# RWKV stage of a hybrid decoder layer: which engine makes the low parts and the second copy, and which bank holds the bonus product

## The chip, the cores and the metric

The kernel runs on one core of a Trainium2 chip. The metric is the device time of one execution in microseconds. Before the change the median of 3 runs is 2224.1 us (2221.66 to 2224.29).

## The reference

One layer of a decoder on a sequence of 1024 tokens with 1024 channels, in float32:

- One input projection `x @ w_in`. Its columns feed RWKV-7 time mixing (8 heads of 64), a sparse attention (8 query heads) and two merge gates of 1024 channels each.
- Time mixing, per head and per token t, with a 64x64 state: `sa = state @ a_t`; `state = state * w_t + sa b_t^T + v_t k_t^T`; `y_t = state @ r_t`. Then a norm per head, and a bonus is added: the sum over the head of `r * k * r_k`, times v.
- Both branches are projected, multiplied by their sigmoid gates, added and projected again; residual and layer norm.
- Cross-attention into 256 memory tokens; residual and layer norm. A gated feed-forward of width 2816 with a convolution of width 3; residual and layer norm.

```
sa = jnp.einsum('bhvk,bhk->bhv', state, a_t)
state = (state * w_t[:, :, None, :] + sa[..., None] * b_t[:, :, None, :]
         + v_t[..., None] * k_t[:, :, None, :])
return state, jnp.einsum('bhvk,bhk->bhv', state, r_t)
```

## The kernel before

**Matmuls in three parts.** Large products run in a reduced float32 format on TensorE. Each operand is split into a high and a low part, and `mm3` (line 194) adds three matmuls: high by high, high weights by low activations, low weights by high activations. `split` (199) makes the parts: ScalarE copies the source into the high part, VectorE subtracts it from the source for the low part. `wload` (211) streams a weight tile this way: a DMA into `raw` (one buffer), then `split` into `wh` and `wl` (two buffers each, so the next load is split as soon as the load before the present one has been used up). `wload` is used in all stages.

**The RWKV stage** (lines 563 to 960) works on four pairs of heads (`hp`) and two halves of the sequence, so on eight units. A half has 8 chunks of 64 tokens. For each unit:

- `operands` (646): decay and key factors. The matmuls `vs` (norm sums), `pw` and `pa` (small projections) and `bc` (the norm brought back, from the tile `w`) feed VectorE, ScalarE and GpSimd. Then the matrix `LT`, and a substitution of 15 steps on VectorE (L729, L730) that inverts its 16x16 blocks.
- `couplings` (746): products `gb` and `gk` masked by VectorE into `GB` and `AMR`; transposes `tr`; and the bonus product `pbo`, which VectorE multiplies by v into `BV`.
- `inverse` (809): the 64x64 inverse from the 16x16 blocks.
- `recurrence` (855): chunk by chunk, `x` on TensorE, copied to `XS` by VectorE; `sa` (the solved rows) on TensorE, whose two halves of 64 partitions are copied to `SV`, one by VectorE (866) and one by ScalarE (867); `z` on TensorE; and the next state `ZV` by VectorE (876), which the next `x` needs.
- `outputs` (879): `psy`, the norm (`vs`, `bc` again) and the bonus.

**Work that fills TensorE.** `large` (512) is a generator for the 13 column pieces of the projection that this stage needs (`prj`) and the 16 pieces of the gates (`gt`). Each piece is a load of 128x1024 and 2 x 8 steps of `mm3`, and the next piece is loaded ahead. The last gates run in the stage of the sparse attention.

**The order.** TensorE's order in this stage is written out by hand: tasks yield an assumed TensorE time and an assumed wait, and a loop (950 to 960) takes the first ready one of recurrences, outputs, inverses, couplings, operands and, last, `large`. The other engines' orders come from a scheduler that works from assumed times; the steps of recurrences and inverses are marked as urgent for it. Every engine then works in its own order, and waits by semaphores.

**PSUM banks** are handed out in turn within a role (563 on): role s has banks 2, 3 and 6 and serves `operands` and `couplings`; role o has bank 7 alone and serves `outputs`; b and c serve inverse and recurrence; g the filling matmuls.

Of the kernel before, what the change touches and what calls it, by code (L numbers as in the profile page):

```python
# [10 lines left out]
F32 = mybir.dt.float32  # L11
# [115 lines left out]
def layer_kernel(ctx: ExitStack, tc, I, out, cst):  # L127
# [42 lines left out]
    def pss(name="pss"):  # L170
        return bank("s", name)
# [4 lines left out]
    def pso(name="pso"):  # L176
        return bank("o", name)
# [18 lines left out]
        PE.matmul(o, lh, rl, start=False, stop=False)  # L196
        PE.matmul(o, ll, rh, start=False, stop=stop)  # L197

    def split(src, h, l):
        S.activation(h, src, AF.Copy)  # L200
        V.tensor_sub(l, src, h.bitcast(F32))  # L201

    class W:
        def __init__(self, ku):
# [3 lines left out]
            u, q = divmod(k, self.ku)  # L208
            return self.h[u][:, q, c:c + m], self.l[u][:, q, c:c + m]

    def wload(pieces, kt=8):

        n = sum(p.shape[1] for p in pieces)
        w = W(min(kt, WUNIT // n))
        for k0 in range(0, kt, w.ku):
            ku = min(w.ku, kt - k0)
            wp = in_turn("w", cur["w"])
            raw = wp.tile([P, ku, n], F32, tag="raw", bufs=1, name="raw")
            h = wp.tile([P, ku, n], F32R, tag="wh", bufs=2, name="wh")
            l = wp.tile([P, ku, n], F32R, tag="wl", bufs=2, name="wl")  # L220
            o = 0
            for p in pieces:
                m = p.shape[1]
                SP.dma_start(raw[:, :, o:o + m], p[k0 * P:(k0 + ku) * P].rearrange("(k p) n -> p k n", p=P))
                o += m
            split(raw, h, l)
            w.h.append(h)
            w.l.append(l)
        return w
# [282 lines left out]
    def large():  # L512

        def load():
            while pq and not may_load(*pq[0]) and not gq:
                yield 0, 0.5
            if pq and may_load(*pq[0]):
                c = pq.pop(0)
                col0 = c[1] * RC + c[0] * P
            elif gq:  # L520
                c = gq.pop(0)
                col0 = GATE0 + c * P
            else:
                return None
            return c, wload([win[:, col0:col0 + P]])

        ahead = yield from load()
        while ahead:
            c, w = ahead
            ahead = yield from load()  # L530
            gate = isinstance(c, int)
            if not gate:
                hp, j = c
                while not may_project(hp, j):
                    yield 0, 0.5
                dst = [LO[:, 0:HALF], LO[:, HALF:T]] if j == 3 else [ex(f"X{a}{j}") for a in range(2)]
                Xs[c] = dst
                last = sm.tile([P, 1], F32, name="last", tag="last", bufs=4)
            for half in range(2):
                ps = pg("gt" if gate else "prj")  # L540
                for k in range(8):
                    mm3(ps, *w.at(k, 0, P), *xT.mov(k, half), k == 0, k == 7)
                    if k < 7:
                        yield L_DENSE, 0, True
                if gate:
                    t = cur["st"].tile([P, HALF], F32, tag="gst", name="gst", bufs=1)
                    S.activation(t, ps, AF.Tanh, scale=0.5)
                    S.dma_start(gscr[c * P:(c + 1) * P, half * HALF:(half + 1) * HALF], t)
                else:
                    shifted(ps, dst[half], j * 4 + hp, half, last)  # L550
                    if half:
                        if j == 3:
                            S.activation(LO[0:64, :], LO[0:64, :], AF.Tanh)
                        projected.add(c)
                yield L_DENSE, 0, False
# [190 lines left out]
    def couplings(me):  # L746

        u, (hp, half) = units[me], divmod(me, 2)
        Xr, E3, ET, BH, KH, BB, KB_, TMP = u.operands
        Xv = Xs[hp, 2][half]  # L750
        AMR = k8("AMR")
        for h, rw in enumerate(rows_h):
            G.tensor_tensor(AMR[rw, :, 1, h, :], r8(Xr[rw]), r8(ET[rw]), op=OP.mult)
            S.activation(AMR[rw, :, 0, h, :], r8(E3[rw]), AF.Copy)

        GB, KS, SV, ZV = k2("GB"), k4("KS"), k4("SV"), k4("ZV")
        u.AMR, u.GB, u.KS, u.SV, u.ZV = AMR, GB, KS, SV, ZV
        if half == 0:
            for h, rw in enumerate(rows_h):
                G.memset(ZV[rw, 0, h, :], 0.0)  # L760
        yield 0, 5.5
        ps = pss("gb").rearrange("p (c t) -> p c t", t=CH)
        for c in range(NC8):
            for h, rw in enumerate(rows_h):
                PE.matmul(ps[rw, c], BH[rw, c * CH:(c + 1) * CH], AMR[rw, c, 1, h, :], start=True, stop=True)
        V.tensor_tensor(GB, ps, bc(gmask[:, CH:P], NC8), op=OP.mult)
        for j in range(2):
            ps = pss("gk").rearrange("p (c a t) -> p c a t", a=2, t=CH)
            for ci in range(4):
                c = 4 * j + ci  # L770
                for h, rw in enumerate(rows_h):
                    PE.matmul(ps[rows_h[1 - h], ci], KH[rw, c * CH:(c + 1) * CH], AMR[rw, c, :, h, :], start=True, stop=True)
            for h in range(2):
                rx = rows_h[1 - h]
                m = gmask[rx].rearrange("p (a t) -> p a t", a=2)[:, None].to_broadcast([64, 4, 2, CH])
                V.tensor_tensor(AMR[rx, 4 * j:4 * j + 4, :, h, :], ps[rx], m, op=OP.mult)
        yield 2.9, 1.0

        for src, flip, dst in ((Xv, 1, ZV), (BB, 0, KS), (KB_, 1, KS)):
            ps = pss("tr").rearrange("p (c n) -> p c n", n=P)  # L780
            for c in range(4):
                PE.transpose(ps[:, c, :], src[:, c * P:(c + 1) * P], ident)
            if src is Xv:

                mv = sm.tile([P, 4, 2], F32, name="vm", tag="vm", bufs=2)
                V.tensor_reduce(mv, ps.rearrange("p c (h d) -> p c h d", h=2), axis=AX.X, op=OP.add)
            for h in range(2):
                ro = rows_h[1 - h] if flip else rows_h[h]
                for q, rq in enumerate(rows_h):
                    o, v = dst[ro, q:NC8:2, h, :], ps[rq, :, h * 64:h * 64 + 64]  # L790
                    if src is Xv:
                        m = mv[rq, :, h][:, :, None].to_broadcast([64, 4, 64])
                        V.scalar_tensor_tensor(o, m, -1.0 / 64, v, op0=OP.mult, op1=OP.add)
                    else:
                        S.activation(o, v, AF.Copy)
                if src is Xv:
                    G.tensor_copy(SV[ro, :, h, :], ZV[ro, :, h, :])
            yield 0.5, 0.8
        yield 0, 2.5
        if me >= 2:  # L800
            while not outputs_[me - 2].done:
                yield 0, 0.5
        u.BV = ec("BV")
        ps = pss("pbo")
        PE.matmul(ps, ones, TMP, start=True, stop=True)
        V.scalar_tensor_tensor(u.BV, ps, 64.0, Xv, op0=OP.mult, op1=OP.mult)
        yield 1.1, 0
# [47 lines left out]
    def recurrence(i):  # L855
        u, (hp, half) = units[i], divmod(i, 2)
        AMR, EE, KS, SV, ZV, WC = u.AMR, u.EE, u.KS, u.SV, u.ZV, u.WC
        for c in range(NC8):
            ps = bank("c", "x")
            PE.matmul(ps[:, 0:P], pair(AMR[:, c, 0]), pair(ZV[:, c]), start=True, stop=True)  # L860
            XS = sm.tile([P, P], F32, name="XS", tag="XS", bufs=2)
            V.tensor_copy(XS, ps[:, 0:P])
            yield 0.35, 0.8
            ps = bank("c", "sa")
            PE.matmul(ps[:, 0:P], pair(EE[:, c]), XS, start=True, stop=True)
            V.tensor_copy(SV[0:64, c, 0, :], ps[0:64, 0:64])
            S.activation(SV[64:128, c, 1, :], ps[64:128, 64:128], AF.Copy)
            yield 0.25, 1.4
            if not (half == 1 and c == NC8 - 1):
                ps = bank("c", "z")  # L870
                PE.matmul(ps[:, 0:P], pair(KS[:, c]), pair(SV[:, c]), start=True, stop=True)
                while c == NC8 - 1 and not couplings_[i + 1].done:
                    yield 0, 0.5
                for h, rw in enumerate(rows_h):
                    dst = ZV[rw, c + 1, h, :] if c < NC8 - 1 else units[i + 1].ZV[rw, 0, h, :]
                    V.scalar_tensor_tensor(dst, ZV[rw, c, h, :], WC[rw, c, :], ps[rw, h * 64:h * 64 + 64], op0=OP.mult, op1=OP.add)
                yield 0.25, 1.2
# [657 lines left out]
```

## Time and profile before

| | before |
|---|---|
| median of 3 runs | 2224.1 us |
| the profiled execution, its own time | 2223.49 us |
| span of the profiled execution | 2221.7 us |
| TensorE busy in the span | 2131.7 us (96%) |
| VectorE busy | 1232.4 us (55%) |
| ScalarE busy | 889.2 us (40%) |
| GpSimd busy | 475.0 us (21%) |

The span goes from the first to the last instruction; the execution's own time is 1.8 us longer. Busy is the time in which an engine has an instruction in work. In the rows further down, PE is TensorE, DVE VectorE, ACT ScalarE, POOL GpSimd. Matmuls overlap their neighbours, so a row's duration is longer than the distance to the next row.

### The profile page before, as it was taken

The page shows a single profiled execution, that of the slowest core. Times are in us where ns is not written, and L with a number is a line of the kernel's source. Part 1 is how long each engine was busy: PE and PEld are TensorE (multiplying, and loading weights), DVE is VectorE, ACT ScalarE, POOL GpSimd, SP SyncE. Part 2 cuts the span into 40 slices and gives each one's busy share as a digit, 9 for nine tenths or more (in the row PEclk, how much of TensorE's full clock was granted, in tenths as well). Part 3 has the DMA queues.
Part 4 walks back from the last instruction along what each step waited for, and adds up shares of the span by engine and source line. Part 5 has one row for each costly group of instructions (what it writes and reads, how often), then busy time and mean ns, then how long its engine had stood idle before and what let it go on. Part 6 is the DMA issues. An engine that isn't in the chain of part 4 may idle for free.

```text
span 2221.7 us, 31651 instructions
## 1 busy us (share of the span) xinstructions
PE 2131.7 (96%) x12301; PEld 1706.0 (77%) x12301; DVE 1232.4 (55%) x2416; ACT 889.2 (40%) x1441; POOL 475.0 (21%) x544
## 2 busy tenths in 40 slices
PE   9989999999999899999899999999999999999997
PEld 7978777777778667756678877788888888888886
DVE  3422576777652787888656535275444434344447
ACT  3433443544533576776523424142322313132232
POOL 2112231333300244444422101030100101000013
PEclk9999999999999999999999999999999999999999
DMA  6544112121223321112252313111111111111102
GB/s 206 152 150 124 49 24 56 36 52 32 62 59 94 110 66 45 42 45 68 72 189 86 123 38 114 39 39 57 38 48 48 54 42 57 39 57 57 57 29 86
DMA packets 196659, 157.91 MB, mean 71 GB/s; under 512 B 49061, under 2 KB 164766, under 8 KB 196510
## 3 DMA queue, kind: packets, MB, share of 16 engines
q1 hardware_dynamic: 184798, 139.10, 21.2%
q10 hardware_dynamic: 11136, 14.68, 2.0%
q0 software_dynamic: 576, 2.10, 0.3%
q8 instruction: 98, 1.61, 0.3%
q14 instruction: 51, 0.42, 0.1%
HBM read 125.86 MB, written 29.98 MB: 70 GB/s over the span
## 4 chain that ended last, share of the span: by engine, by line
PE 47%; DVE 5%; ACT 2%; DMA 1%; issue 1%; POOL 0%; SPq 0%; ACTq 0%; DVEq 0%; POOLq 0%
PE up L196 7%; PE up L197 7%; PE up L195 7%; PE dn L195 4%; PE dn L197 4%; PE dn L196 4%; PE op L195 2%; PE op L197 1%; PE op L196 1%; PE xq L195 1%; PE xq L196 1%; PE xq L197 1%; DVE acc L1334 1%; ACT acc L1333 1%; DVE bs L1327 1%
## 5 line engine op out<-in xcount | busy, mean ns | idle before, releaser
L200 ACT ACTIVATE wh<-raw 128x1024 fp32r<-128x1024 f32 (+1 forms) x160 | 168.8, 1055 | 474.9 <-PE dn L197 138.1
L201 DVE TENSOR_TENSOR wl<-raw,wh 128x1024 fp32r<-128x1024 f32 (+1 forms) x160 | 198.1, 1239 | 282.5 <-ACT wh L200 281.5
L196 PE MATMUL up<-nTl,wh 128*128 128x512 f32 x704 | 276.5, 393 | 0.0
L197 PE MATMUL up<-nTh,wl 128*128 128x512 f32 x704 | 276.4, 393 | 0.0
L195 PE MATMUL up<-nTh,wh 128*128 128x512 f32 x704 | 276.4, 393 | 0.0
L1458 DVE SCALAR_TENSOR_TENSOR cv<-up,pv,cv 128x511 f32<-128x511 f32 (+1 forms) x176 | 131.5, 747 | 145.4 <-ACT cv L1456 143.4
L1482 POOL TENSOR_TENSOR cv<-cv 128x512 f32<-128x512 f32 x44 | 56.8, 1291 | 630.9 <-DVE cl L1462 413.5
L196 PEld LDWEIGHTS up<-nTl,wh 128*128 128x128 f32 x704 | 132.3, 188 | 29.6
L195 PEld LDWEIGHTS up<-nTh,wh 128*128 128x128 f32 x704 | 132.2, 188 | 29.6
L197 PEld LDWEIGHTS up<-nTh,wl 128*128 128x128 f32 x704 | 132.2, 188 | 29.6
L1106 POOL TENSOR_TENSOR pl<-pe,ph 128x512 fp32r<-128x512 f32 x87 | 114.3, 1317 | 161.3 <-ACT ph L1105 97.3
L195 PE MATMUL dn<-wh,gT 128*128 128x512 f32 x352 | 138.1, 393 | 0.2 <-ACT wh L200 0.2
L197 PE MATMUL dn<-wh,gT 128*128 128x512 f32 x352 | 137.5, 391 | 0.0
L196 PE MATMUL dn<-wl,gT 128*128 128x512 f32 x352 | 136.9, 389 | 0.0
L1493 DVE SCALAR_TENSOR_TENSOR acc<-acc,dn 128x512 f32<-128x512 f32 x96 | 65.5, 686 | 95.5 <-PE dn L197 94.9
L1456 ACT ACTIVATE cv<-up,pv 128x512 f32<-128x512 f32 x88 | 68.5, 778 | 117.2 <-PE up L197 117.2
L195 PE MATMUL gt<-xTh,wh 128*128 128x512 f32 x256 | 113.0, 441 | 0.5 <-DVE nm L1074 0.5
L197 PE MATMUL gt<-xTh,wl 128*128 128x512 f32 x256 | 102.3, 399 | 0.0
L196 PE MATMUL gt<-xTl,wh 128*128 128x512 f32 x256 | 101.9, 398 | 0.0
L1335 POOL TENSOR_TENSOR acc<-acc,lngb 128x1024 f32<-128x1024 f32 x21 | 50.4, 2401 | 206.0 <-DVE acc L1334 129.8
L1105 ACT ACTIVATE ph<-pe 128x512 fp32r<-128x512 f32 (+1 forms) x148 | 90.2, 627 | 6.9 <-POOL macc L1223 4.6
L195 PE MATMUL prj<-xTh,wh 128*128 128x512 f32 x208 | 90.5, 435 | 2.2 <-ACT wh L200 2.2
(365 smaller groups left out, 5092.2 us busy)
## 6 DMA issues: line engine op xcount, KB each, us to landing
raw<-in_ffn_w_up_dram SPq DMA_DIRECT2D x88, 256.0 KB
raw<-in_w_in_dram SPq DMA_DIRECT2D x33, 512.0 KB
raw<-in_ffn_w_down_dram SPq DMA_DIRECT2D x22, 512.0 KB
gscr<-gst ACTq DMA_DIRECT2D x32, 256.0 KB
rawn<-nst SPq DMA_DIRECT2D x16, 256.0 KB
raw<-in_xa_wk_dram SPq DMA_DIRECT2D x8, 512.0 KB
raw<-in_xa_wv_dram SPq DMA_DIRECT2D x8, 512.0 KB
gl<-gscr SPq DMA_DIRECT2D x16, 256.0 KB
```

The lines of the kernel that those rows point to most:

```text
L195: PE.matmul(o, lh, rh, start=start, stop=False)
L196: PE.matmul(o, lh, rl, start=False, stop=False)
L197: PE.matmul(o, ll, rh, start=False, stop=stop)
L200: S.activation(h, src, AF.Copy)
L201: V.tensor_sub(l, src, h.bitcast(F32))
L1105: S.activation(h, e, AF.Copy)
L1106: in_turn("l", LTURN)(l, e, h.bitcast(F32), op=OP.subtract)
L1335: (V if tt == NT - 1 else G).tensor_tensor(r[:, c], r[:, c], gb[:, 1, c], op=OP.add)
L1456: S.activation(c, ps, AF.Identity, scale=pc("cw2", ci), bias=pc("ffn_conv_b", ci))
L1458: V.scalar_tensor_tensor(c[:, s:], ps[:, :HALF - s], pc(nme, ci), c[:, s:], op0=OP.mult, op1=OP.add)
L1482: G.tensor_tensor(c[0], c[0], c[1], op=OP.mult)
L1493: V.scalar_tensor_tensor(v, v, 1.0 if f else ALPHA, ps, op0=OP.mult, op1=OP.add)
```

## The change

Three edits. `split` and `wload` get a parameter for the engine that makes the low part, and `large` passes GpSimd; all other callers keep VectorE. In `recurrence` the second half of the solved rows is copied by VectorE, as the first is. In `couplings` the bonus product takes its bank from role o instead of role s.

```diff
-    def split(src, h, l):
+    def split(src, h, l, low=V):
         S.activation(h, src, AF.Copy)
-        V.tensor_sub(l, src, h.bitcast(F32))
+        low.tensor_tensor(l, src, h.bitcast(F32), op=OP.subtract)
...
-    def wload(pieces, kt=8):
+    def wload(pieces, kt=8, low=V):
...
-            split(raw, h, l)
+            split(raw, h, l, low)
...
-            return c, wload([win[:, col0:col0 + P]])
+            return c, wload([win[:, col0:col0 + P]], low=G)
...
-        ps = pss("pbo")
+        ps = pso("pbo")
         PE.matmul(ps, ones, TMP, start=True, stop=True)
         V.scalar_tensor_tensor(u.BV, ps, 64.0, Xv, op0=OP.mult, op1=OP.mult)
...
             V.tensor_copy(SV[0:64, c, 0, :], ps[0:64, 0:64])
-            S.activation(SV[64:128, c, 1, :], ps[64:128, 64:128], AF.Copy)
+            V.tensor_copy(SV[64:128, c, 1, :], ps[64:128, 64:128])
```

## Rows read from the trace of the kernel before

**Rows 1.** Busy time: stretch, its length, PE, PEld, DVE, ACT, POOL, PEclk, DMA, GB/s

```profile
200.00:732.00 532.00, 501.02 (x4597) 402.67 (x4596) 324.95 (x810) 229.20 (x401) 135.95 (x155) 0.98 0.23 60
```

**Rows 2.** TensorE's waits from 200 to 760 us: total us, times, longest

```profile
PE z L871 <- ACT SV L867: 5.1, 7, 1.5
```

**Rows 3.** Timeline of TensorE: start, us, instruction, count, idle before and its releaser

```profile
276.44 2.07 PE L668 MATMUL pa<-LO,lw 64*128 64x512 f32 x2 [3.65 <-DVE BV L806]
279.81 1.11 PE L635 MATMUL bc<-ident,w 128*128 128x128 f32 x4 [1.30 <-ACT w L629]
281.57 0.63 PE L197 MATMUL prj<-xTh,wl 128*128 128x512 f32 x1
...
394.23 0.40 PE L197 MATMUL prj<-xTh,wl 128*128 128x512 f32 x1
```

**Rows 4.** Busy time and clock (PEclk) from within the wait of pa on

```profile
275.50:285.70 10.20, 7.96 (x18) 5.33 (x19) 7.08 (x12) 5.68 (x9) 6.61 (x8) 0.50 0.31 70
```

**Rows 5.** VectorE's groups, 200 to 760 us: count, busy us, mean ns, idle before

```profile
L201 DVE TENSOR_TENSOR wl<-raw,wh 128x1024 fp32r<-128x1024 f32 x30 | 36.6, 1221 | 35.0 <-ACT wh L200 34.7
...
L866 DVE COPY SV<-sa 64x64 f32<-64x64 f32 x64 | 13.6, 213 | 31.6 <-PE sa L865 31.3
```

**Rows 6.** Timelines of VectorE and ScalarE: copies of the solved rows

```profile
393.53 0.22 DVE L866 COPY SV<-sa 64x64 f32<-64x64 f32 x1 [0.58 <-PE sa L865]
...
395.30 0.22 ACT L867 ACTIVATE SV<-sa 64x64 f32<-64x64 f32 x1
...
484.16 0.22 DVE L866 COPY SV<-sa 64x64 f32<-64x64 f32 x1 [0.58 <-PE sa L865]
```

**Rows 7.** Timeline of TensorE: five waits of z

```profile
314.90 0.49 PE L871 MATMUL z<-SV,KS 128*128 128x128 f32 x2 [0.49 <-ACT SV L867]
...
395.57 0.49 PE L871 MATMUL z<-SV,KS 128*128 128x128 f32 x2 [0.94 <-ACT SV L867]
...
481.16 0.49 PE L871 MATMUL z<-SV,KS 128*128 128x128 f32 x2 [0.36 <-ACT SV L867]
...
485.07 0.49 PE L871 MATMUL z<-SV,KS 128*128 128x128 f32 x2 [0.95 <-ACT SV L867]
...
593.25 0.49 PE L871 MATMUL z<-SV,KS 128*128 128x128 f32 x2 [0.24 <-ACT SV L867]
```

**Rows 8.** Timeline of VectorE around the wait of pa

```profile
273.64 1.21 DVE L201 TENSOR_TENSOR wl<-raw,wh 128x1024 fp32r<-128x1024 f32 x1
...
275.70 0.69 DVE L806 SCALAR_TENSOR_TENSOR BV<-pbo,X 128x512 f32<-128x512 f32 x1
...
276.57 0.15 DVE L623 TENSOR_SCALAR rs<-vs 128x8 f32<-128x8 f32 x1
```

**Rows 9.** Timeline of ScalarE ahead of bc

```profile
279.14 0.62 ACT L629 ACTIVATE w<-rs 128x512 f32<-128x512 f32 x1
```

**Rows 10.** Timeline of TensorE: a wait of pbo

```profile
580.32 1.12 PE L805 MATMUL pbo<-TMP,csr 128*128 128x512 f32 x2 [0.85 <-DVE ZV L793]
```

**Rows 11.** GpSimd's groups on the page: count, busy us, mean ns, idle before

```profile
L1106 POOL TENSOR_TENSOR pl<-pe,ph 128x512 fp32r<-128x512 f32 x87 | 114.3, 1317 | 161.3 <-ACT ph L1105 97.3
...
L1335 POOL TENSOR_TENSOR acc<-acc,lngb 128x1024 f32<-128x1024 f32 x21 | 50.4, 2401 | 206.0 <-DVE acc L1334 129.8
```

**Rows 12.** Timelines of GpSimd and TensorE at the first load

```profile
204.58 0.96 POOL L737 MEMSET EE<- 128x1024 f32 x1
...
206.03 0.50 PE L197 MATMUL prj<-xTh,wl 128*128 128x512 f32 x1 [0.53 <-DVE wl L201]
```

**Rows 13.** VectorE's substitution: its group (200 to 760 us), and timelines beside GpSimd

```profile
L729 DVE TENSOR_TENSOR stmp<-DB,LB 64x1 f32<-64x1 f32 (+14 forms) x120 | 43.6, 363 | 8.0 <-DMA LB<-d 5.3
...
313.83 1.35 POOL L676 TENSOR_TENSOR E<-CU,E 128x512 f32<-128x512 f32 x1 [2.00 <-DVE CU L673]
314.32 1.02 DVE L729 TENSOR_TENSOR stmp<-DB,LB 64x81 f32<-64x81 f32 x1
...
628.32 1.21 DVE L201 TENSOR_TENSOR wl<-raw,wh 128x1024 fp32r<-128x1024 f32 x1
```

## The prediction

> **What bounds the kernel now.** I read the busy times by stretch first. In the stretch from 200 to 732 us, the RWKV stage, TensorE is busy 501 of 532 us; VectorE is busy 325 us and GpSimd 136 us [rows 1]. TensorE is the bound, its order there is written out by hand, and so at most 31 us can be won: the time in which it stands still. The second view is TensorE's waits. The reader is to look for the waits that end on something the change touches. One line is for the copy of the solved rows by ScalarE, 5.1 us in 7 waits [rows 2]. The largest single wait is in the timeline: the matmul pa stands 3.65 us until VectorE has read the bonus product BV, and bc stands 1.30 us more [rows 3]. The third view is the granted clock around that place: in the 10.2 us that begin within this standstill, at 275.5, the clock is at 0.50, the lower of its two levels, 1.2 GHz [rows 4]. There a matmul of 512 columns shows 0.63 us; at the full clock, at 394.23, the same one shows 0.40 us [rows 3].
>
> **Part 1, the second copy of the solved rows goes from ScalarE to VectorE (64 times).** Now VectorE copies the upper half (64 rows, mean 213 ns [rows 5]), ScalarE starts when that is done, and the product z waits for ScalarE. Where ScalarE is free the two follow each other at once, and nothing is won. Where it is not, z waits: at 393.53 VectorE has made its copy in 0.22 us, but ScalarE's starts at 395.30, behind the work already in its queue, and z stands 0.94 us [rows 6, 7]. With both copies on VectorE, the second one ends some 0.43 us after the first began. z's five waits of 0.49, 0.94, 0.36, 0.95 and 0.24 us [rows 7] would then go, of the fourth 0.43 only, because VectorE itself was late there (its copy began at 484.16 [rows 6]). The sum is 0.49 + 0.94 + 0.36 + 0.43 + 0.24 = 2.5 us. Bounds: 0, if something else is late next, and 5.1 us, all of these waits [rows 2]. I take -2.5. What is late next is ZV, VectorE's own step after z; it follows z by a fixed distance, so it moves up with it. ScalarE gets 64 short instructions less, which I cost at nothing: it is not the bound.
>
> **Part 2, the bonus product pbo moves from the three banks of role s to the outputs' bank.** One use less in the rotation by three: pa no longer gets pbo's bank and no longer waits for BV. But the gain is not 3.65 us, because the next matmul, bc, waits for w, and w has its own chain: VectorE's rs at 276.57 [rows 8], then ScalarE's root of it, and w itself at 279.14 [rows 9], just ahead of bc. That pa comes early moves none of these, so I give the bank alone nothing here. But rs stands in VectorE's queue behind wl, 1.21 us [rows 8]; that instruction leaves with part 3, so 1.2 us. The low clock costs 12 matmuls of the projection that run in it 12 x (0.63 - 0.40) = 2.8 us; the standstill becomes shorter but doesn't go, so I take half, 1.4 us. Together -2.6. Bounds: 0, if bc still begins at 279.81, and 3.65 + 1.30 + 2.8 = 7.75 us, if nothing stands still. A second gain of the same edit: at 580.32 pbo stands 0.85 us for its bank of role s, still read by ZV [rows 10]; in the outputs' bank nothing reads at that time: -0.85, between 0 and 0.85. The new wait is pbo behind the outputs of two halves earlier (their last read, a product by VectorE), and the next outputs behind BV. In the order by hand the couplings wait for these outputs anyway, and the next outputs come only after a whole recurrence, so I cost it at 0; without that cover it would be one VectorE product, 0.69 us as BV's [rows 8], in each of six halves: 4 us.
>
> **Part 3, the low parts of 29 streamed loads go from VectorE to GpSimd.** The code has 13 pieces of the projection and 16 gates; of the 30 rows of 1.22 us [rows 5], the last belongs to the merge. 28 of the 29 lie in the stage. On GpSimd a subtraction of 128x512 takes 1.32 us, and an addition of 128x1024 takes 2.40 us [rows 11], so 2.4 to 2.6 us; I take 2.5.
> - Where the low part is waited for at once: the first load. TensorE stands 0.53 us for wl and goes on at 206.03 [rows 12]. On GpSimd it ends 1.2 us later if it starts at once, and 2.2 us later if it stands behind the memset that ends at 205.54 [rows 12]. I take +1.5. For the other loads a whole load's matmuls lie between (16 steps of three, which the order by hand counts at 0.69 us: 11 us), and 2.5 us are hidden; if GpSimd's queue held wl for more than about 8 us, that cover would be gone and each further us would be one of TensorE's. The next load's DMA, which SP issues when raw is free, comes up to 1.3 us later and has the same cover.
> - What VectorE wins: 28 x 1.22 = 34.2 us less, 64 x 0.213 = 13.6 us more (part 1), so 20.6 us less in its queue. What it loses: VectorE products with both inputs in SBUF are held while GpSimd reads. The row: a step of the substitution of 64x81 takes 1.02 us beside GpSimd's product (313.83 to 315.18), where the mean of all these steps is 0.36 us [rows 13]. Eleven of the loads come while the substitution (120 such steps [rows 13]) or the products of operands run; the first is the wl of 273.64 [rows 8], the last that of 628.32 [rows 13]. If each holds VectorE for the full 2.5 us, that gives back 27.5 us. So VectorE's queue changes by -20.6 to +6.9 us. TensorE sees about a tenth of it (31 us of standstill for 325 us of VectorE [rows 1]): -2.0 to +0.7. I take the middle, -0.7.
>
> The page SBUF — State Buffer (section "Who interferes with whom") of the Trainium skill states that a VectorE instruction with two SBUF inputs and a GpSimd instruction that reads SBUF exclude each other for the whole of the one that came first. By that rule the change is worse than its count of instructions: it swaps a hold of 1.2 us for one of 2.5. This trace agrees: the step of 1.02 us ends at 315.34, just behind GpSimd's 315.18 [rows 13].
>
> **The sum.** -2.5 - 2.6 - 0.85 - 0.7 + 1.5 = -5.15 us. The profiled execution took 2223.5 us (span 2221.7 and 1.8 around it), so 2218.3 us. The profiled execution is 0.6 us under the median of 2224.1; against that the forecast is 5.8 us, 0.26%, faster. About 0.2%, 4.4 us, is what a measurement of this kernel can tell from no change.
>
> **Rivals.**
> 1. The hold decides, and the kernel is slower. Place: the eleven loads above; a step of the substitution at the head of VectorE's queue holds the recurrence's copies behind it. Price: 2.5 - 1.22 = 1.28 us per load, 14 us in all; half of it seen by TensorE, 7 us. With -2.5 - 0.85 + 2.2 from the other parts: 2223.5 + 5.85 = 2229.3 us. It outweighs them from 1.15 us, one load of the eleven, and makes the kernel 0.2% slower than the median from 6.2 us, five loads. For it: the 1.02 us row. Against it: VectorE spends 1.2 us on each of these loads today, and the recurrence's own instructions read PSUM.
> 2. The waits come back at the next place, and nothing can be measured. VectorE works in order, the substitution stands between the recurrence's steps, and what z gains ZV loses. Half of part 1 (-1.25), nothing at bc, -0.85 at pbo, +1.5 at the first load: -0.6, so 2222.9 us. For it: part 1 wins only where ScalarE was busy, 5 waits of 64 copies. Against it: z and pa stand in TensorE's own fixed order, and time won there is lost again only if another chain is already late.
>
> **How the numbers follow.** Forecast 0.50, of which 0.45 is faster by over 0.2% and 0.05 within; its own range is 2213 to 2221. Rival 1 has 0.19, all of it slower. Rival 2 has 0.31, within 0.2%. So faster 0.45, same 0.36, slower 0.19. For the range, all upper bounds together (-5.1 - 7.75 - 0.85 - 2.0 + 1.2 = -14.5) give 2209; I leave out a little there and the upper half of rival 1: 2210 to 2228.
>
> **What would show it.** Part 1: the line of waits "z for SV of ScalarE" is gone, and no line "z for SV of VectorE" of over 3 us stands in its place. Part 2: pa follows pw at once, bc begins before 279.8 us counted from the same start of the stage, and the stretch at clock 0.50 there is shorter. Part 3: wl on GpSimd at 2.4 to 2.6 us, the first prj standing 1.7 to 2.7 us for it, later ones not at all; the mean of the substitution's products, 363 ns now [rows 13], not above 500. Wrong would be: that mean much higher with more waits for XS or ZV (rival 1), waits for wl after the first load, or the time from 200 us to the end of the stage unchanged though z and pa don't wait.

## The result, and the profile after

The changed kernel takes 2250.2 us (median of 4 runs, 2245.6 to 2250.5); the kernel before, beside it, 2223.0 us (4 runs, 2221.7 to 2224.3). The ratio is 1.0117 with a 95% interval of 1.0102 to 1.0132. So it is 27 us slower, where the forecast was 5.8 us faster. Its profiled execution took 2250.1 us, with a span of 2248.3 us. One run of a kernel told below (y4_proj, 2614.1 us at a mean granted clock of 0.75) is left out of the medians.

The RWKV stage, from 200 us to the same last matmul (columns as in [rows 1]):

```profile
200.00:758.00 558.00, 508.96 (x4595) 410.44 (x4595) 330.62 (x848) 213.75 (x337) 200.98 (x183) 0.96 0.21 57
```

The stage is 26 us longer, so nearly the whole loss is here. TensorE's matmuls are the same. It stands still for 558.0 - 509.0 = 49.0 us, 18 us more than the 31.0 us of [rows 1], and the same matmuls are busy for 7.9 us more, because the mean granted clock of the stage fell from 0.98 to 0.96. VectorE has lost all its low parts, and is still busy for 331 us, not less than before.

TensorE's waits in the stage (total us, times, longest), after, and then two lines of before that [rows 2, 3] don't show:

```profile
PE x L860 <- DVE ZV L876: 18.1, 15, 2.6
PE bc L635 <- ACT w L629: 8.1, 1, 8.1
PE z L871 <- DVE SV L867: 6.4, 6, 2.0
PE kT L985 <- DMA kld<-rawn: 5.2, 2, 4.0
PE prj L197 <- POOL wl L201: 1.7, 1, 1.7
```

```profile
PE x L860 <- DVE ZV L876: 7.6, 12, 1.4
PE kT L985 <- DMA kld<-rawn: 3.1, 1, 3.1
```

The matmul x waits 10.5 us more for VectorE's state ZV. z waits 6.4 us for VectorE where it waited 5.1 us for ScalarE [rows 2]. The standstill of pa and bc (3.65 and 1.30 us [rows 3]) has become one of 8.1 us at bc.

The groups of the stage after, to be read against [rows 5, 13] (count, busy us, mean ns, idle before), and then the line of L614 before. L614 is a VectorE operation with two SBUF inputs and a single column:

```profile
L201 POOL TENSOR_TENSOR wl<-raw,wh 128x1024 fp32r<-128x1024 f32 x29 | 69.9, 2410 | 133.6 <-ACT wh L200 122.2 <-DMA EE<-d 11.2
L729 DVE TENSOR_TENSOR stmp<-DB,LB 64x1 f32<-64x1 f32 (+14 forms) x120 | 52.8, 440 | 8.5 <-DMA LB<-d 5.3
...
L862 DVE COPY XS<-x 128x128 f32<-128x128 f32 x64 | 18.4, 287 | 24.4 <-PE x L860 24.0
...
L614 DVE SCALAR_TENSOR_TENSOR X<-last,pv,X 128x1 f32<-128x1 f32 x12 | 9.1, 756 | 0.0
```

```profile
L614 DVE SCALAR_TENSOR_TENSOR X<-last,pv,X 128x1 f32<-128x1 f32 x12 | 4.2, 350 | 0.0
```

GpSimd's low part takes the 2.4 us that was forecast. The substitution's products rose from 363 ns [rows 13] to 440, and L614, one column wide, from 350 to 756. Copies out of PSUM (L862) did not change: 289 ns before, 287 after. What a single one of these products does, and to whom, is in the timeline of the kernel after (start, us, instruction, idle before and its releaser):

```profile
597.09 2.37 POOL L201 TENSOR_TENSOR wl<-raw,wh 128x1024 fp32r<-128x1024 f32 x1
597.25 0.38 PE L871 MATMUL z<-SV,KS 128*128 128x128 f32 x2
597.45 2.40 DVE L729 TENSOR_TENSOR stmp<-DB,LB 64x225 f32<-64x225 f32 x1
599.88 0.69 DVE L806 SCALAR_TENSOR_TENSOR BV<-pbo,X 128x512 f32<-128x512 f32 x1
600.49 0.37 DVE L730 TENSOR_REDUCE DB<-stmp 64x15 f32<-64x225 f32 x1
600.78 0.56 DVE L876 SCALAR_TENSOR_TENSOR ZV<-ZV,WC,z 64x64 f32<-64x64 f32 x2
...
601.49 0.46 PE L860 MATMUL x<-ZV,AMR 128*128 128x128 f32 x2 [2.37 <-DVE ZV L876]
```

z is done at 597.6, but the product at the head of VectorE's queue takes 2.40 us, until GpSimd's subtraction is over (another of the same form, undisturbed, takes 0.53). ZV stands behind it and behind BV, and x waits 2.37 us. At the projections of the decay the same happens to rs; the last line is the same step of the substitution in the kernel before:

```profile
276.23 2.33 POOL L201 TENSOR_TENSOR wl<-raw,wh 128x1024 fp32r<-128x1024 f32 x1
...
276.08 2.67 DVE L729 TENSOR_TENSOR stmp<-DB,LB 64x100 f32<-64x100 f32 x1
...
282.76 0.15 DVE L623 TENSOR_SCALAR rs<-vs 128x8 f32<-128x8 f32 x1
...
276.57 0.69 PE L668 MATMUL pa<-LO,lw 64*128 64x512 f32 x1
...
285.75 1.12 PE L635 MATMUL bc<-ident,w 128*128 128x128 f32 x4 [8.06 <-ACT w L629]
```

```profile
270.82 0.32 DVE L729 TENSOR_TENSOR stmp<-DB,LB 64x100 f32<-64x100 f32 x1
```

pa follows pw at once. But rs stands behind the rest of the substitution, as it did before, and one step of it now takes 2.67 us in place of 0.32; bc waits for w, which is made from rs. Counted from the start of pbo, which is at 274.24 here and at 269.85 before, rs runs 1.8 us later than before (at 282.76, against 276.57 [rows 8]), and bc begins 1.6 us later (285.75, against 279.81 [rows 3]).

### The profile page after: what moved, and what is told of

It reads as the page before. It is cut to its first block, busy times and chain, and to the rows that moved or that the text cites. A ratio compares the mean times of both kernels' runs of the same rounds, so it can differ in the third digit from the quotient of the medians.

```text
span 2248.3 us, 31726 instructions
## 1 busy us (share of the span) xinstructions
PE 2139.4 (95%) x12301; PEld 1713.2 (76%) x12301; DVE 1234.6 (55%) x2451; ACT 872.8 (39%) x1377; POOL 542.7 (24%) x573
## 4 chain that ended last, share of the span: by engine, by line
PE 46%; DVE 5%; ACT 2%; DMA 1%; issue 1%; POOL 0%; SPq 0%; ACTq 0%; DVEq 0%; POOLq 0%
PE up L196 7%; PE up L197 7%; PE up L195 7%; PE dn L195 4%; PE dn L197 4%; PE dn L196 3%; PE op L195 2%; PE op L197 1%; PE op L196 1%; PE xq L195 1%; PE xq L196 1%; PE xq L197 1%; DVE acc L1334 1%; ACT acc L1333 1%; DVE bs L1327 1%
## 5 line engine op out<-in xcount | busy, mean ns | idle before, releaser
L201 DVE TENSOR_TENSOR wl<-raw,wh 128x1024 fp32r<-128x1024 f32 (+1 forms) x131 | 162.7, 1243 | 245.3 <-ACT wh L200 244.8
L201 POOL TENSOR_TENSOR wl<-raw,wh 128x1024 fp32r<-128x1024 f32 x29 | 69.9, 2410 | 133.6 <-ACT wh L200 122.2
```

Source lines behind the costliest of these rows:

```text
L201: low.tensor_tensor(l, src, h.bitcast(F32), op=OP.subtract)
```

## Experiments

Three theories were on the table. H: GpSimd's reading of SBUF holds VectorE's products with two SBUF inputs. Q: GpSimd's fuller queue makes its own work late. O: the scheduler has laid out VectorE's queue anew, and that order is worse. The expectations also name rival C (the second copy on VectorE costs) and rival K, or edge theory (only the first load and the end of the stage cost). Times are medians of 3 to 12 runs beside 13 to 20 runs of the kernel before on the same chip (medians 2223.2 to 2224.2 us); the losses told below are the differences to those.

| kernel | us | over before | ratio to before (95%) |
|---|---|---|---|
| x1_low: part 3 alone | 2247.0 | +23.8 | 1.0115 (1.0100 to 1.0131) |
| x2_copy: part 1 alone | 2229.9 | +6.8 | 1.0035 (1.0022 to 1.0048) |
| x3_bank: part 2 alone | 2221.4 | -1.8 | 0.9993 (0.9984 to 1.0003) |
| x4_copy_bank: parts 1 and 2 | 2227.2 | +4.0 | 1.0017 (1.0005 to 1.0029) |
| y1_nohold: part 3, memsets | 2231.6 | +8.1 | 1.0040 (1.0026 to 1.0053) |
| y5_light: part 3, short | 2224.1 | +0.5 | 1.0000 (0.9991 to 1.0010) |
| y2_cut: part 3, in four pieces | 2246.5 | +22.9 | 1.0088 (1.0061 to 1.0114) |
| z3_extra: before + extra subtraction | 2251.8 | +28.4 | 1.0135 (1.0115 to 1.0155) |
| z4_extra_mem: before + extra memsets | 2234.8 | +11.4 | 1.0053 (1.0032 to 1.0074) |
| y3_gates: part 3 for the 16 gates | 2234.7 | +11.2 | 1.0050 (1.0035 to 1.0065) |
| y4_proj: part 3 for the 13 pieces | 2240.2 | +16.0 | 1.0074 (1.0058 to 1.0089) |
| w1_edges: part 3 without 3 loads | 2238.7 | +14.5 | 1.0070 (1.0057 to 1.0083) |
| z1_swap: copies exchanged | 2235.0 | +11.6 | 1.0056 (1.0034 to 1.0077) |
| z2_act: both copies by ScalarE | 2223.6 | +0.2 | 0.9999 (0.9988 to 1.0009) |
| w2_act_bank: the same, and part 2 | 2222.4 | -1.8 | 0.9995 (0.9984 to 1.0006) |

**Which part?** Each part put alone into the kernel before, and parts 1 and 2 together; the edits are the hunks of the change.

> Part 3 alone: the 29 low parts on GpSimd, nothing else changed. Theory H (the hold: GpSimd's subtraction of 2.4 us keeps VectorE's products with two SBUF inputs waiting, and the recurrence's copies stand behind them): 16 to 27 us slower than before, with the mean of the substitution's products (363 ns before) over 440 ns and the wait of x for ZV (7.6 us before) over 13 us. Rival C (the second copy on VectorE is what costs: 64 more instructions in VectorE's order, and the scheduler's order around them): 0 to 6 us slower. Rival K (only the two places at the edge of the stage cost, the first load and the transfer kld behind GpSimd's queue at the stage's end): 5 to 8 us slower, all of it before 210 us and after 720 us.

> Part 1 alone: both halves of the solved rows copied by VectorE. Theory H: 1 to 4 us faster (the 2.5 us of waits of z that ScalarE caused). Rival C: 12 to 25 us slower, with z's waits now on VectorE's copy and over 5 us, and more waits of x for ZV. Rival K: 1 to 4 us faster, as theory H.

> Part 2 alone: the bonus product in the outputs' bank. All theories: between 3 us faster and 1 us slower; pa follows pw at once, bc still waits for w until about the same time (a wait of 7 to 8 us in place of 3.65 and 1.30), and the 0.85 us wait of pbo at 580 us is gone.

> Parts 1 and 2 without part 3. Theory H: 1 to 6 us faster than before. Rival C: 10 to 25 us slower. Rival K: 1 to 6 us faster; H and K are told apart by where x1_low loses its time. If this one and x1_low are both far from what their sum needs (together 26 us), the parts act on each other through VectorE's order.

Part 3 alone costs 23.8 us, part 1 alone 6.8 us, part 2 alone -1.8 us. Their sum, 28.8 us, is close to the 27.2 us that all three cost. With part 3 alone L729's mean is 420 ns and x waits 10.1 us for ZV, less than H had said, while the time is what H had said. For x2_copy and x4_copy_bank every theory was wrong: two had them 1 to 6 us faster, the third 10 to 25 us slower, and they are 6.8 and 4.0 us slower.

**Is it the reading?** Two kernels with part 3's streamed loads keep GpSimd as busy, or half as busy, without the reading of 128x1024. Most of the low parts are left out in them, so they measure time alone.

```diff
-        low.tensor_tensor(l, src, h.bitcast(F32), op=OP.subtract)
+        # y1_nohold: 8 columns, then 2.4 us of memsets
+        G.tensor_tensor(l[:, :, 0:1], src[:, :, 0:1], h[:, :, 0:1].bitcast(F32), op=OP.subtract)
+        [G.memset(l[:, 0:n].bitcast(F32), 0.0) for n in (8, 8, 3)]
+        # y5_light: one memset, then 64 columns
+        G.memset(l.bitcast(F32), 0.0)
+        G.tensor_tensor(l[:, :, 0:8], src[:, :, 0:8], h[:, :, 0:8].bitcast(F32), op=OP.subtract)
```

> Part 3 alone, but GpSimd spends its 2.5 us per load on memsets of wl (which read nothing) behind a subtraction of only 8 columns; the low parts of the weights are left out. TensorE's order is that of part 3 alone (2247.0 us), VectorE's differs in one substitution. Theory H (GpSimd's reading of SBUF holds VectorE's products, and that makes the +24 us): the mean of the products L729 falls from 420 ns to under 375, L614 from 796 to under 450, and the time to 2222-2231 us. Theory O (the new order of VectorE's instructions makes it): the products fall the same, but the time stays at 2240-2248. Theory Q (GpSimd's own queue, 70 us fuller, makes it): stays at 2240-2248, and TensorE waits for GpSimd's operands as in part 3 alone.

> Part 3 alone, with one memset (0.96 us) and a subtraction of 64 columns (estimate 0.3 us) on GpSimd per load; most of the low parts are left out. Per load GpSimd has 1.3 us in place of 2.4, VectorE none. Orders as in the kernel with memsets alone. H: 2220-2229 us, within 3 us of the kernel with memsets of 2.5 us. Q: clearly below that kernel, by 8 us or more. O: both at 2240 or more.

The stage in x1_low, then the stage and the substitution in y1_nohold (columns as in [rows 1, 13]):

```profile
200.00:755.00 555.00, 513.08 (x4596) 411.09 (x4595) 311.82 (x784) 230.47 (x401) 201.90 (x183) 0.96 0.22 58
```

```profile
200.00:736.50 536.50, 505.30 (x4577) 407.30 (x4577) 291.18 (x783) 229.69 (x400) 203.46 (x267) 0.97 0.22 58
```

```profile
L729 DVE TENSOR_TENSOR stmp<-DB,LB 64x1 f32<-64x1 f32 (+14 forms) x120 | 39.6, 330 | 7.6 <-DMA LB<-d 4.7
```

GpSimd is as busy (203 and 202 us) and VectorE has the same instructions, 20.6 us less to do. The loss is 15.7 us smaller (8.1 for 23.8; 2231.6 us is just above H's range, and 8 us under the 2240 that O and Q had). So H carries up to two thirds of part 3. Not all of it need be the reading, for by the traces VectorE's order differs at two substitutions, at 263 to 280 and 617 to 640 us of y1_nohold. Between them it is the same, and there, from the z at 344.50 us (350.28 in x1_low) to the x at 616.27 us (631.65), x1_low takes 9.6 us longer.

In this pair the reading doesn't act where H had looked for it. TensorE's waits in x1_low, then in y1_nohold:

```profile
PE x L860 <- DVE ZV L876: 10.1, 11, 1.9
PE z L871 <- ACT SV L867: 7.5, 9, 1.9
```

```profile
PE x L860 <- DVE ZV L876: 10.0, 11, 1.9
PE z L871 <- ACT SV L867: 4.0, 7, 1.1
```

The wait for ZV is the same with and without it. What the reading lengthens is z's wait for SV, sa's for XS (4.5 us against 1.8) and pa's for BV (3.4 against 0.4). In the pair of the next test it does lengthen the wait for ZV (12.7 against 8.2 us), so which step is hit goes by the kernel.

The other 8 us stay as long as GpSimd is that busy, and are gone with 1.3 us per load (y5_light): that is Q's share, told apart below. H's 2220 to 2229 us for y5_light came true, its "within 3 us" of the memsets did not; Q's "8 us or more" below them was missed by half a microsecond. O, which had both at 2240 or more, falls for part 3: with nearly all of VectorE's new order and a light GpSimd the time is that of before.

**The same from the other side.** VectorE keeps every wl, and GpSimd does extra work behind each streamed load, into `raw`, which nobody reads any more.

```diff
         V.tensor_sub(l, src, h.bitcast(F32))
+        G.tensor_tensor(src, src, h.bitcast(F32), op=OP.subtract)   # z3_extra
+        [G.memset(src[:, 0:n], 0.0) for n in (8, 8, 4)]             # z4_extra_mem
```

> The kernel before (VectorE makes all low parts), and after each of the 29 streamed loads GpSimd subtracts wh from raw once more, into raw, which nobody reads after that: 2.4 us of GpSimd reading two SBUF tiles, and no instruction but the next load's DMA waits for it. Theory H (hold): L729's mean rises from 363 to over 400 ns, x and z wait longer, and the time rises by 8 to 20 us, to 2231-2243. Rival (the loss of part 3 comes from wl being on a chain through GpSimd, not from the reading): under 3 us more than before, 2220-2226, since no wl waits for GpSimd here.

> The same, but GpSimd's extra work is memsets of raw (2.4 us in three instructions, nothing read). H: L729's mean stays under 375 ns; the time is at least 8 us under the kernel with the extra subtraction, at 2222-2230, where what is above before is the price of GpSimd's fuller queue (that queue stood for 7.5 us between memsets of 2.5 us and a load of 1.3 us). Rival: equal to the kernel with the extra subtraction within 3 us.

The stages of z3_extra and z4_extra_mem, and one z of the recurrence in each:

```profile
200.00:764.00 564.00, 513.70 (x4581) 409.76 (x4580) 345.89 (x812) 229.66 (x400) 199.51 (x183) 0.95 0.21 56
463.33 0.49 PE L871 MATMUL z<-SV,KS 128*128 128x128 f32 x2
```

```profile
200.00:742.00 542.00, 504.50 (x4606) 405.83 (x4606) 326.81 (x812) 231.21 (x403) 203.85 (x239) 0.97 0.22 59
449.33 0.49 PE L871 MATMUL z<-SV,KS 128*128 128x128 f32 x2
```

Reading instead of writing costs VectorE 19.1 us and the kernel 17.0 us, though no wl waits for GpSimd here. This settles H against its rival, and the order is no way out: VectorE's is the same in both up to 458 us, and the same z, counted from the first matmul of the stage (at 203.41 and 205.23 us), is by then 15.8 us later in z3_extra. z3_extra came out higher than its range and z4_extra_mem too: the fuller queue alone costs 11.4 us.

**Shorter holds.**

```diff
-        low.tensor_tensor(l, src, h.bitcast(F32), op=OP.subtract)
+        [G.tensor_tensor(l[:, q:q + 2], src[:, q:q + 2], h[:, q:q + 2].bitcast(F32), op=OP.subtract) for q in (0, 2, 4, 6)]
```

> Part 3 alone, with GpSimd's subtraction of 128x1024 cut into four of 128x256 (estimate 0.65 us each, 2.6 us per load). All engines' orders are those of part 3 alone. H: a VectorE product can get in between two pieces and is held 0.65 us at most, so L729's mean falls to 370-400 ns and the time to 2230-2240 us. O and Q: L729's mean may fall, but the time stays within 3 us of 2247, for Q rather above it (four fixed costs per load in place of one).

H's figure failed: the median did not fall, though its four runs lie far apart (2236.1 to 2251.1 us, and the profile is of the slowest). Groups of y2_cut with two of its loads, then the group of x1_low that answers to L690:

```profile
L201 POOL TENSOR_TENSOR wl<-raw,wh 128x256 fp32r<-128x256 f32 x112 | 84.1, 781 | 123.3 <-ACT wh L200 122.7 <-POOL ZV L760 0.4
...
L690 DVE TENSOR_TENSOR KH<-KP,E 128x512 f32<-128x512 f32 x8 | 9.6, 1200 | 6.9 <-POOL KP L686 6.8
...
213.30 2.83 POOL L201 TENSOR_TENSOR wl<-raw,wh 128x256 fp32r<-128x256 f32 x4 [4.41 <-ACT wh L200]
...
330.55 4.53 POOL L201 TENSOR_TENSOR wl<-raw,wh 128x256 fp32r<-128x256 f32 x4 [1.29 <-ACT wh L200]
```

```profile
L690 DVE TENSOR_TENSOR KH<-KP,E 128x512 f32<-128x512 f32 x8 | 7.0, 879 | 1.2 <-POOL KP L686 1.2
```

VectorE's products got shorter (L729 395 ns), but GpSimd needs longer. Most loads take 2.8 us in four pieces in place of 2.4, which is the price of the cuts; six of 28 take 3.2 to 4.5 us. At 330.55 us three of VectorE's operations with two SBUF inputs (L687, L614, L688) run between the pieces. GpSimd's next product KP comes late, and VectorE waits 6.8 us for it, not 1.2; x waits 13.5 us for ZV, not 10.1, and z 4.9 for SV, not 7.5. The loss changed its place.

**Which loads?** Part 3 for the gates alone, for the pieces of the projection alone, and for all but the first load and the last two gates.

```diff
+ low=G if isinstance(c, int) else V          # y3_gates (y4_proj the other way round)
+ low=V if c in ((0, 1), 14, 15) else G       # w1_edges
```

> Part 3 for the 16 gate pieces only; the 13 pieces of the projection keep VectorE. H: the share of the loss goes with the loads that meet two-input products; the gates fill TensorE behind the recurrences, where the substitution and the operands run as well: 2232-2240 us. O: VectorE's order stands halfway between the two kernels, 2230-2240 too; apart from H by L729's mean: 390-400 under H, and no row over 1 us larger without a GpSimd row over it. Edge theory (the loss is the first load and the change of stage at 720 us): the first load is on VectorE again, so the drift at 210 us is under 1 us, and the one at 720 stays: 2227-2230.

> Part 3 for the 13 pieces of the projection only; the 16 gates keep VectorE. If the losses of loads add up (part 3 alone +24 us, gates alone +11), this has +13: 2234-2240 us, with the first load's delay of 2 to 4 us at 210 us, and no jump at the change to the sparse attention at 720 us, since no load there is GpSimd's. Order theory (each new order of VectorE's queue throws its own number): the two partial kernels don't add up, and this one may stand anywhere from 2223 to 2245.

> Part 3 alone, but the first load and the last two gates keep VectorE: 26 of 29 loads on GpSimd, order of all other instructions nearly that of part 3 alone (2247.0 us). Queue theory at the two edges: the first prj waits under 0.6 us for wl, and the drift at 210 us is under 1 us in place of 4.3; the DMA of kld, which GpSimd issues, no longer stands behind a wl at the change of stage, kT waits 3.1 us as before and the jump at 720 us (+5) is under 1.5: 2237-2241 us. Hold theory alone: the loss shrinks by 3 of 29 loads, 2.5 us: 2243-2246.

16 gates cost 11.2 us, 13 pieces 16.0 us; together 27.2, a little over the 23.8 of all. So the loss goes with the loads, as H and Q have it. (For y3_gates H and O had named the same times; the mean of L729, 380 ns, lies under the 390 to 400 that H had.) The three loads at the edges cost 9.3 us (23.8 less 14.5), as Q had said, not 2.5. What they do at the first load and at the change to the sparse attention, in the kernel after (the first pair answers to [rows 12]):

```profile
204.27 2.35 POOL L201 TENSOR_TENSOR wl<-raw,wh 128x1024 fp32r<-128x1024 f32 x1 [17.09 <-ACT wh L200]
...
206.68 0.50 PE L197 MATMUL prj<-xTh,wl 128*128 128x512 f32 x1 [1.69 <-POOL wl L201]
...
737.97 1.29 POOL L902 TENSOR_TENSOR Y<-Y,BV 128x512 f32<-128x512 f32 x1 [9.58 <-ACT Y L901]
740.76 2.39 POOL L201 TENSOR_TENSOR wl<-raw,wh 128x1024 fp32r<-128x1024 f32 x1 [1.50 <-ACT wh L200]
743.10 1.07 POOL L979 DMA_DIRECT2D kld<-rawn  x1
...
749.18 1.24 PE L985 MATMUL kT<-ident,kld 128*128 128x128 f32 x8 [3.98 <-DMA kld<-rawn]
```

and in w1_edges:

```profile
205.22 0.51 PE L197 MATMUL prj<-xTh,wl 128*128 128x512 f32 x1 [0.52 <-DVE wl L201]
...
731.95 1.28 POOL L902 TENSOR_TENSOR Y<-Y,BV 128x512 f32<-128x512 f32 x1 [9.57 <-ACT Y L901]
733.17 1.07 POOL L979 DMA_DIRECT2D kld<-rawn  x1
```

GpSimd issues the DMA of kld. With a wl in its queue, that DMA is issued 743.10 - 739.26 = 3.8 us after the last Y, and the first kT waits 3.98 us for it; without, it is issued at once, and that kT doesn't wait. y1_nohold (edges without reading, 8.1 us) and w1_edges (reading without edges, 14.5 us) nearly add up to x1_low (23.8).

**The copies.**

```diff
+ S.activation(SV[0:64, c, 0, :], ps[0:64, 0:64], AF.Copy)         # z1_swap, z2_act, w2_act_bank
+ V.tensor_copy(SV[64:128, c, 1, :], ps[64:128, 64:128])           # z1_swap
+ ps = pso("pbo")                                                  # w2_act_bank
```

> The kernel before with the two copies of the solved rows exchanged: ScalarE copies the half of rows 0 to 63, VectorE that of rows 64 to 127. Each engine has as many instructions as before, of the same length; only the scheduler's order of VectorE and ScalarE differs in places. Load theory (part 1 alone cost 7 us because VectorE has 13.6 us more to do in the stage): within 3 us of before. Order theory (part 1's 7 us come from where the scheduler puts long VectorE instructions between the steps of the recurrence, whatever the load): the time may differ from before by 3 to 8 us in either direction.

> The kernel before with both copies of the solved rows on ScalarE, the opposite of part 1: VectorE has 13.6 us less. Load theory: x waits less than 7.6 us for ZV, and the time is 1 to 6 us under before. Order theory: ZV's waits and the time go either way by up to 7 us; z's waits for ScalarE grow over 5.1 us because both copies then stand in ScalarE's queue.

> No part 3, part 2 as it is, and the opposite of part 1: both copies of the solved rows on ScalarE. Both copies on ScalarE alone measured as before; the bank alone -1.8 us, within the noise. If they add: 2220-2223 us, at most 0.2% faster than before, which 5 rounds may just tell. If the bank's gain of 2 us is taken back by another order: 2223-2228.

z1_swap did not test what it was meant to. The two copies run one after the other, so in it VectorE's copy waits for ScalarE's:

```profile
DVE SV L867 <- ACT SV L866: 38.2, 29, 2.6
```

VectorE's queue stands 38.2 us there, where before it stood 31.3 us at its first copy, for sa; and z waits 10.1 us for VectorE's copy, where it waited 5.1 us for ScalarE's. The kernel is 11.6 us slower, more than either theory had. z2_act takes 13.6 us of copies from VectorE and gains nothing: z's waits for SV nearly go (1.2 us), but x waits 11.3 us for ZV in place of 7.6. Load theory, which had it 1 to 6 us faster, fails; so does the order theory's longer wait of z for ScalarE. w2_act_bank can't be told from before, so no version that beats the kernel before was found.

## Why the prediction was wrong, point by point

**The step that failed is in part 3: "TensorE sees about a tenth of it", which made -0.7 us.** The forecast turned VectorE's time into TensorE's by a ratio of totals, 31 us of standstill to 325 us of VectorE [rows 1]. The bounds for VectorE (-20.6 to +6.9 us) were sound: it came out at +5.7 (331 against 325 us). The conversion was not: part 3 was to cost +0.8 us with the first load, and cost 23.8. Between x1_low and y1_nohold VectorE differs by 20.6 us and the loss by 15.7, three quarters; between z3_extra and z4_extra_mem by 19.1 and 17.0 us. A held product is not spread over the stage. It is up to 2.3 us at one place at the head of an in-order queue, and ZV, XS, SV, BV or rs stand behind it. For the time that VectorE saves the tenth was nearer. In y5_light VectorE has 34 us less (291 against 325), and the last Y of GpSimd comes 4.3 us earlier (at 709.29 against 715.74, counted from the first matmul of the stage at 202.65 and 204.77), an eighth; but the DMA of kld, behind a wl again, only 2.2 us (712.62 against 716.97), and the end of the kernel not at all.

The Trainium skill's page SBUF — State Buffer, section "Who interferes with whom", has the rule of H: a VectorE instruction with two SBUF inputs contends with a GpSimd instruction that reads SBUF, and not with one that only writes it. The runs agree on both halves: L729 at 420 ns beside subtractions, and 330 ns beside memsets. The prediction cited the rule and gave it 7 us and a chance of 0.19. Its 14 us, before it halved them, are near the 15.7 measured. (Its break-even points, one load and five, leave that half out; with it they are two and ten.) Against it stood "the recurrence's own instructions read PSUM". They do, and L862 kept its time; but they queue behind instructions that are held.

**The first load, +1.5 us.** TensorE waited 1.69 us for wl, as forecast (1.7 to 2.7). But the edges together cost 9.3 us. The DMA of kld in GpSimd's queue was not in the sum. And a standstill cost more than itself: right behind the wait at the first load the 128x512 matmul takes 0.63 us (at 207.68) and only at 210.66 0.40 again, as at the two clocks of [rows 3].

**The clock as a second term.** Of the stage's 26 us, 18 are standstill and 8 are the same matmuls taking longer, at a mean granted clock of 0.96 in place of 0.98. In x1_low it is 11 and 12. The forecast had this term only once, at pa.

**Part 1, -2.5 us.** z's waits fell from 5.1 to 2.7 us in x2_copy, the forecast gain almost to the tenth. What failed is a later sentence, "it follows z by a fixed distance, so it moves up with it": x waited 13.4 us for ZV, 5.8 more. With 2.0 us more of q for DD and 1.1 of sa for XS, less the 2.4 won, that makes 6.5, near the 6.8 us lost. The timelines of x2_copy and then of the kernel before show one place:

```profile
483.96 0.22 DVE L866 COPY SV<-sa 64x64 f32<-64x64 f32 x1 [0.58 <-PE sa L865]
484.19 0.23 DVE L867 COPY SV<-sa 64x64 f32<-64x64 f32 x1
484.45 1.23 DVE L673 TENSOR_TENSOR_SCAN CU<-csr,E 128x512 f32<-128x512 f32 x1
485.71 0.59 DVE L876 SCALAR_TENSOR_TENSOR ZV<-ZV,WC,z 64x64 f32<-64x64 f32 x2
...
486.45 0.77 PE L860 MATMUL x<-ZV,AMR 128*128 128x128 f32 x2 [1.42 <-DVE ZV L876]
```

```profile
485.60 0.59 DVE L876 SCALAR_TENSOR_TENSOR ZV<-ZV,WC,z 64x64 f32<-64x64 f32 x2 [1.23 <-PE z L871]
486.22 1.23 DVE L673 TENSOR_TENSOR_SCAN CU<-csr,E 128x512 f32<-128x512 f32 x1
```

In the kernel before, VectorE stood idle between that copy and ZV, and the scan came behind ZV. Here the scheduler has put the scan of 1.23 us between them. That is rival 2's sentence, "what z gains ZV loses", and more than that. Why the scheduler chose such places was not tried, and whether another order would keep the 2.4 us stays open.

**Part 2, -3.45 us.** x3_bank measured -1.8 us, within the noise. pa follows pw at once and pbo's wait is gone, but bc begins at 279.90 us, as before (279.81 [rows 3]): w's own chain sets it, as the prediction said of the bank alone. The 1.2 us that rs was to gain with part 3 became a loss of 1.8 us: wl is gone from ahead of it, but a step of the substitution is held there for 2.3 us. So the standstill grew to 8.1 us, and the 1.4 us of the low clock were not won either.

**What would show it.** The prediction's signs of being wrong were the right ones: more waits for ZV, and a wait of z for VectorE of over 3 us in place of the one for ScalarE. One was set too high: L729's mean was to exceed 500 ns, and 440 were enough.

## What to carry to other kernels

Don't convert an engine's saved or added time into kernel time by the ratio of totals. Ask for each added instruction what stands behind it in its queue at that place, and for each removed one whether anything was waiting. Before a two-input elementwise operation goes to GpSimd, look for VectorE's two-input products at the same time: a subtraction of 2.4 us cost some 0.5 us of kernel time by its reading alone (up to 15.7 us for 29 loads), and cutting it in four did not lower the time. A queue that also issues DMAs needs their times in the sum.

## What the runs showed of the hardware that was not expected

- A product of a single column (L614, 128x1) is held as a large one is: 350 ns mean before, 756 after, 921 in z3_extra, and 279 and 259 in the two kernels with memsets. In after, x1_low and z3_extra no L614, L687 or L729 that began within one of GpSimd's subtractions ended before that subtraction did. The one at 276.08 us began 0.15 us ahead of the subtraction by the trace, and was held too.
- The hold runs both ways. In y2_cut GpSimd's four pieces took 2.8 us for most loads, and 4.53 us beside three of VectorE's operations with two SBUF inputs.
- GpSimd's memsets of 128x1024 don't hold VectorE's products: L729's mean is 330 and 358 ns in the two kernels with memsets, against 363 before.
